# Expert rows written to a buffer of their own and added in the last stage, slots read from DRAM tables, down biases added once per token

## The chip, the cores and the metric

One core of a Trainium2 chip runs the whole program. The metric is the time of one execution in microseconds of the device; lower is better. A run of the kernel before is repeated on the same chip, and the median counts. One execution was also taken with the hardware profiler, and the trace comes from that one.

The names of the engines in the profile: PE does matrix products and transposes, DVE works on vectors, ACT does activations and copies with a scale, POOL does small work and issues the indirect transfers, SP issues loads.

## The reference, cut to what matters

A float32 transformer of two blocks on 512 tokens of 1024 columns. The second block has 32 experts, of which every token takes 4. What the change touches is the expert part and what follows it:

```python
xn = rms_norm_2(h, ffn_norm)
logits = xn @ w_router + b_router
top_vals, top_idx = lax.top_k(logits, 4)
gates = softmax(top_vals)
# for each expert e, on the rows of the tokens that chose it
gt = minimum(xb @ w_gate[e] + b_gate[e], 7.0)
up = clip(xb @ w_up[e] + b_up[e], -7.0, 7.0)
hdn = (up + 1.0) * (gt * sigmoid(1.702 * gt))
y = (hdn @ w_down[e] + b_down[e]) * gate
h = h + sum over a token's four experts of y
gate = sigmoid(rms_norm_2(h, ple_gate_norm) @ w_ple_gate)
h = h + gate * rms_norm_2(p @ w_ple_proj, ple_post_norm)
```

## The kernel before, in words

Every large product is made in three matmuls on a pair of reduced operands (`mm3`, lines 314 to 316): high x high, low weight x high, high weight x low. A weight part is 128 rows of 1024 columns: one load on SP (line 296), a cast to the high part `whi` on ACT (line 285), a subtraction that leaves the low part `wlo` on DVE (line 285), and six matmuls of 512 columns on PE.

**Routing.** `attended_rows(tt)` ends the attention's output for a token tile of 128 (tiles 3, 2, 1, 0 in turn), writes it to `base` in DRAM on ACT's queue, and `route(tt)` (line 1293) finds the four experts: transposes, the router matmuls (line 1309), `rstd` on POOL (lines 320, 323), `lg`, the top four, `chosen`, and a running count of tokens per expert, which is each token's slot (`slot_of`). `info` keeps for every token and expert the gate in two parts, the token number and the row's norm in two parts. After the last tile `first_rows` makes the token numbers `gi` of expert 0, and POOL gathers its rows from `base` (line 1424).

**Slots.** The list of tokens of an expert comes from a product: a one-hot matrix of the slots (`one_hot`, DVE, line 1419) times `info` (`slot_products`, four small matmuls, line 1489), copied out and turned into the gate and the row numbers (`slot_columns`). Experts 0 and 1 are done ahead of the loop, the other 30 in groups of four inside it, at every fourth expert.

**The expert loop** (line 1586). An expert has 112 slots. Its 24 steps `q` are: q 0 to 7 the gate product into `pg`, q 8 to 15 the up product into `pu`, q 16 to 23 the down product of the expert before into `pd`. At q 0, 8 and 16 `add_bias` (line 1465) starts the sum with the bias, by two matmuls of 512 columns on `pick`. `turned` transposes the gathered rows `xg` after q 15 and the hidden rows `uc` after q 23 (line 1511, eight transposes each); `halves_of` splits them into `xe` (q 17) and `he` (q 1). `limited_up` and `gated_rows` make `uc` on DVE at q 18 and 19; for expert 0, which has no q 16 to 23, they stand at its end. `put_rows` scales the down product by the gate (`yt`, ACT) and adds it to the tokens' rows of `base`, by an indirect transfer that accumulates (POOL, line 1527). `fetch` keeps four parts ahead.

The order on PE, DVE and ACT inside the loop is the order of the program text, made fast by dependences after the loop. SP loads in the order of the parts, as raw buffers come free. POOL issues the gathers and the writes in its own fixed order.

**The last stage** loads each tile's finished row from `base` (`hk`, line 1751) and the product of p (`ee`), transposes it, multiplies by the gate weights (four tiles of 48 matmuls), and writes out. Two runs of warming matmuls (`keep_warm`, line 364) keep PE busy between the loop and the last stage.

## Time and profile before

| what | us |
|---|---|
| median of 3 runs (2210.2 to 2211.66) | 2210.4 |
| profiled execution, its own time | 2211.0 |
| span of the profiled execution | 2209.3 |
| PE busy | 2116.2 (96%) |
| DVE busy | 1650.9 (75%) |
| ACT busy | 1357.8 (61%) |
| POOL busy | 207.0 (9%) |

The span runs from the first to the last recorded instruction; what lies around it, 1.7 us, is in the run's own time. The busy share of PE is a mean over stages: the first block and the attention up to about 860 us, the routing up to 924, the expert loop up to 2127, and the last stage. A row of the timeline gives the start, the busy time, engine, line, operation, the tile written and those read, and in brackets the idle time before with what ended it. Matmuls overlap, so the step from one start to the next is their pace, not their busy time. Lines are those of the kernel before.

### The profile page before, as it was taken

The numbers are of one execution on the slowest core, as the hardware profiler recorded it, in microseconds if no ns is written. First come the engines' busy times: TensorE is split into PE (matmuls) and PEld (weight loads), VectorE is DVE, ScalarE is ACT, GpSimd is POOL, SyncE is SP. The second block draws the span as 40 slices with busy tenths as digits, with TensorE's granted clock in tenths as the row PEclk, the third lists the DMA queues.
The fourth block names the chain that finished last, engine by engine and source line by source line (L and its number), as shares of the span: only waits on it lengthen the run. The fifth ranks groups of instructions, "written<-read, shape, count | busy, mean of one in ns | idle before, by whom it ended". The sixth has DMA issues, their size and how long they took to land. (4 is left out here: it accounts for less than half of the span.)

```text
span 2209.3 us, 29934 instructions
## 1 busy us (share of the span) xinstructions
PE 2116.2 (96%) x10458; PEld 1670.1 (76%) x10459; DVE 1650.9 (75%) x2291; ACT 1357.8 (61%) x1841; POOL 207.0 (9%) x325
## 2 busy tenths in 40 slices
PE   9999999999999889799999999999999999999997
PEld 7777788888878777567777777777777777777776
DVE  6688772223576756778888989898889888888852
ACT  5666652222564644367777777777777777777851
POOL 0000110000003332100000000000000000000010
PEclk9999999999999989899999999999999999999999
DMA  6401744333664025689999999999999999999751
GB/s 212 152 30 30 263 145 154 96 96 123 217 210 130 11 96 205 240 294 347 358 338 368 335 364 342 361 344 355 345 357 342 360 352 344 352 357 350 265 165 38
DMA packets 159977, 543.75 MB, mean 246 GB/s; under 512 B 23107, under 2 KB 26179, under 8 KB 159820
## 3 DMA queue, kind: packets, MB, share of 16 engines
q1 hardware_dynamic: 138816, 500.63, 62.9%
q0 software_dynamic: 8192, 16.80, 3.6%
q10 hardware_dynamic: 12812, 24.35, 3.2%
q8 instruction: 84, 1.38, 0.3%
q14 instruction: 73, 0.60, 0.1%
HBM read 525.93 MB, written 28.33 MB: 251 GB/s over the span
## 5 line engine op out<-in xcount | busy, mean ns | idle before, releaser
L285 DVE TENSOR_TENSOR wlo<-wraw,whi 128x1024 fp32r<-128x1024 f32 x923 | 1101.2, 1221 | 315.5 <-ACT whi L285 288.2
L285 ACT CAST whi<-wraw 128x1024 fp32r<-128x1024 f32 x923 | 955.6, 1051 | 407.0 <-PE pw L316 243.7
L314 PE MATMUL pw<-whi,xe 128*112 128x512 f32 x1024 | 405.8, 396 | 0.2 <-ACT xe L285 0.2
L316 PE MATMUL pw<-whi,xe 128*112 128x512 f32 x1024 | 402.4, 393 | 1.1 <-DVE xe L285 1.1
L315 PE MATMUL pw<-wlo,xe 128*112 128x512 f32 x1024 | 402.0, 393 | 0.0
L316 PEld LDWEIGHTS pw<-whi,xe 128*112 128x112 f32 x1024 | 178.6, 174 | 60.1 <-DVE xe L285 1.6
L315 PEld LDWEIGHTS pw<-wlo,xe 128*112 128x112 f32 x1024 | 179.3, 175 | 55.6
L314 PEld LDWEIGHTS pw<-whi,xe 128*112 128x112 f32 x1024 | 178.8, 175 | 56.0 <-ACT xe L285 0.4
L315 PE MATMUL pw<-wlo,he 128*112 128x512 f32 x512 | 203.4, 397 | 18.1 <-DVE wlo L285 18.1
L314 PE MATMUL pw<-whi,he 128*112 128x512 f32 x512 | 202.0, 394 | 0.4 <-ACT he L285 0.4
L316 PE MATMUL pw<-whi,he 128*112 128x512 f32 x512 | 201.0, 393 | 0.0
L315 PEld LDWEIGHTS pw<-wlo,he 128*112 128x112 f32 x512 | 89.3, 174 | 61.9 <-DVE wlo L285 36.5
L314 PEld LDWEIGHTS pw<-whi,he 128*112 128x112 f32 x512 | 89.2, 174 | 29.2 <-ACT he L285 0.8
L1527 POOL DMA_INDIRECT base<-yt,gi x32 | 54.2, 1694 | 595.8 <-ACT yt L1583 595.8
L316 PEld LDWEIGHTS pw<-whi,he 128*112 128x112 f32 x512 | 89.3, 174 | 26.3 <-DVE he L285 0.4
L1424 POOL DMA_INDIRECT xg<-normed,gi x31 | 32.6, 1051 | 530.3 <-PE tr L1511 530.3
L320 POOL TENSOR_SCALAR rstd<-ss 128x1 f32<-128x1 f32 (+1 forms) x68 | 25.0, 368 | 608.2 <-DVE ss L865 387.4
L314 PE MATMUL pa<-x2T,whi 128*128 128x512 f32 (+1 forms) x200 | 72.6, 364 | 0.1
L315 PE MATMUL pa<-x2T,whi 128*128 128x512 f32 (+1 forms) x200 | 72.7, 364 | 0.0
L316 PE MATMUL pa<-x2T,wlo 128*128 128x512 f32 (+1 forms) x200 | 72.6, 363 | 0.0
L1467 PE MATMUL pw<-bias,pick 128*112 128x512 f32 x192 | 65.2, 421 | 0.0
L314 PE MATMUL pb<-whi,x3T 128*128 128x256 f32 x192 | 56.0, 292 | 0.0
(540 smaller groups left out, 3656.5 us busy)
## 6 DMA issues: line engine op xcount, KB each, us to landing
wraw<-in_we_gate_dram SPq DMA_DIRECT2D x256, 512.0 KB, 5.8
wraw<-in_we_up_dram SPq DMA_DIRECT2D x256, 512.0 KB, 6.6
wraw<-in_we_down_dram SPq DMA_DIRECT2D x256, 512.0 KB, 6.9
wraw<-in_w_gu_dram SPq DMA_DIRECT2D x44, 512.0 KB, 3.7
wraw<-in_w_down_dram SPq DMA_DIRECT2D x44, 512.0 KB, 3.9
wraw<-in_w_out_dram SPq DMA_DIRECT2D x24, 512.0 KB, 6.1
wraw<-in_w_v_dram SPq DMA_DIRECT2D x10, 512.0 KB, 4.0
wraw<-in_w_uv_dram SPq DMA_DIRECT2D x8, 512.0 KB, 4.3
```

Of the source, the lines that this page charges most:

```text
L285: return nc.scalar.copy(hi, src), nc.vector.tensor_tensor(out=lo, in0=src, in1=hi.bitcast(F32), op=ALU.subtract)
L314: nc.tensor.matmul(o, a[0], b[0], start=start, stop=False)
L315: nc.tensor.matmul(o, a[0], b[1], start=False, stop=False)
L316: W["mm"] = nc.tensor.matmul(o, a[1], b[0], start=False, stop=stop)
L320: ins = nc.gpsimd.tensor_scalar(out=r[:, :w], in0=ss, scalar1=1.0 / n, scalar2=eps, op0=ALU.mult, op1=ALU.add)
L1424: nc.gpsimd.indirect_dma_start(out=xg[:CAP], out_offset=None, in_=normed if e else base, in_offset=bass.IndirectOffsetOnAxis(ap=slots[e][1 ...
L1467: nc.tensor.matmul(ps[:CAP, c * 512:(c + 1) * 512], pick[:, j % 2, e:e + 1].to_broadcast([P, CAP]), bias[:, j // 2, c * 512:(c + 1) * 512] ...
L1527: nc.gpsimd.indirect_dma_start(out=base, out_offset=bass.IndirectOffsetOnAxis(ap=ap, axis=0), in_=y_, in_offset=None, bounds_check=S - 1, ...
```

## The change

Four things are changed, and some are moved with them.

1. `put_rows` writes its rows plainly to `ybuf`, 2048 rows, four for each token (`store_rows`); nothing accumulates. The last stage loads a token's four rows (`yb`) beside the row of `base` and adds them, on DVE and, for tiles 1 to 3, one addition of each half on POOL.
2. Experts 2 to 31 get their slots from DRAM. 16 tables are set to zero early on SP; after each tile's routing POOL scatters 128 entries of 16 bytes (gate, token, row number) into one table for each of the four choices; SP loads all 16 back, and `finish_table` sums them on DVE in expert 1 at q 3. The one-hot products stay for experts 0 and 1 only.
3. The down bias leaves the loop: the gates are transposed once (expert 2, q 10) and multiplied by all down biases for each token tile in the last stage (`add_down_biases`).
4. `uc` of expert 0 is made at q 0 and 1 of expert 1, and every `uc` is transposed at q 6 of the next expert and split at q 8. The gather of expert 2 stands at q 4 of expert 1. The load of `g_ffn_norm` moves to a pool of its own, behind the attention. Five pools are released at other places.

```diff
+        ybuf = dram.tile([4 * S, D], F32, name="ybuf")
+
+        tables = [dram.tile([P * NE, 4], F32, name=f"table{j}") for j in range(4 * NT)]
+        zeros = mixq.tile([P, 4 * NE], F32, name="zeros")
+        nc.gpsimd.memset(zeros, 0.0)
+        for t in tables:
+            nc.sync.dma_start(t.rearrange("(s e) c -> s (e c)", e=NE), zeros)
...
+        entry = rt.tile([P, NT, 4, 4], F32, name="entry")
+        nc.gpsimd.memset(entry, 0.0)
+        nc.vector.tensor_copy(entry[:, :, :, 1], tok1[:, :, None].to_broadcast([P, NT, 4]))
+        nc.vector.tensor_copy(entry[:, :, :, 2], row)
+        gate_of = rt.tile([P, NT, NE], F32, name="gate_of")
+
+        gateT = rt.tile([P, S], F32R, name="gateT")
...
+            e2 = rp.tile([P, 4, NE], F32, tag="eq2", name="eq2", bufs=1)
+            nc.vector.tensor_tensor(out=e2, in0=eq, in1=slot_of[:, tt, None, :].to_broadcast([P, 4, NE]), op=ALU.mult)
+            at = rp.tile([P, 4], F32, tag="at", name="at", bufs=2)
+            nc.vector.reduce_sum(at, e2, axis=AX)
+            nc.vector.scalar_tensor_tensor(out=place[:, tt], in0=at, scalar=float(NE), in1=ixf, op0=ALU.mult, op1=ALU.add)
...
+        for j, t in enumerate(tables):
+            nc.gpsimd.indirect_dma_start(out=t, out_offset=bass.IndirectOffsetOnAxis(ap=place[:, j // 4, j % 4:j % 4 + 1], axis=0), in_=entry[:, j // 4, j % 4], in_offset=None,
+                                         bounds_check=P * NE - 1, oob_is_err=False)
...
+        def prepare_slots(e):
+            row_column(info[:, :, e, 0], float(e), early)
+            pt = ps_tr()
+            oh = one_hot(e) if e else oh0[0]
             for tt in range(NT):
-                W["pick"] = nc.tensor.matmul(pt[:CAP, 6 * j:6 * j + 6], oh[:, tt], info[:, tt, e], start=tt == 0, stop=tt == NT - 1)
-
-        def slot_columns(pt, e0, n):
-            sl = early.tile([P, NB, 6], F32, name="sl", bufs=2)[:CAP, :n]
-            nc.vector.tensor_copy(sl.rearrange("p j c -> p (j c)"), pt[:CAP, :6 * n])
-            *cols, last = slot_rows(early, sl, n, 4, CAP, e0 == 0)
-            for j in range(n):
...
+        def table_slots():
+
+            tab = early.tile([P, NE, 4], F32, name="tab")
+            sums = []
+            for h in range(2):
+                t = row_tile("tabs").rearrange("p (j f) -> p j f", j=8)
+                for j in range(8):
+                    nc.sync.dma_start(t[:, j], tables[8 * h + j].rearrange("(s e) c -> s (e c)", e=NE))
+                sums.append(t)
+
+            def finish():
+                flat = tab.rearrange("p e c -> p (e c)")
+                part = early.tile([P, 4 * NE], F32, name="tab2")
+                for o, t in zip((flat, part), sums):
+                    nc.vector.reduce_sum(o, t.rearrange("p j f -> p f j"), axis=AX)
+                nc.vector.tensor_tensor(out=flat, in0=flat, in1=part, op=ALU.add)
+                gi, si, _ = rows_of(early, tab[:, :, 1], tab[:, :, 2], NE)
+                for e in range(2, NE):
+                    slots[e] = (tab[:CAP, e, 0:1], gi[:CAP, e:e + 1], si[:CAP, e:e + 1], None)
+
+            return finish
 
         def turned(a):
 
...
-        def add_rows(y_, ap):
-
-            nc.gpsimd.indirect_dma_start(out=base, out_offset=bass.IndirectOffsetOnAxis(ap=ap, axis=0), in_=y_, in_offset=None,
-                                         bounds_check=S - 1, oob_is_err=False, compute_op=ALU.add)
+                scale_rows(xg[:CAP, cs], xg[:CAP, cs], slots[0][3], gpre[:CAP, cs])
+
+        def store_rows(y_, ap):
+            nc.gpsimd.indirect_dma_start(out=ybuf, out_offset=bass.IndirectOffsetOnAxis(ap=ap, axis=0), in_=y_, in_offset=None,
...
         for e in range(NE):
-            if e + 1 < NE:
-                gather(e + 1)
-            batch = list(range(e + 2, min(e + 2 + NB, NE))) if e % NB == 0 else []
-            ohs, pts, pslot = {}, None, None
+            pts, pgate = None, None
             for q in range(24 if e else 16):
                 fetch(at["i"] + 4)
+                if e == 1 and q == 3:
+                    finish_table()
+                if q == (4 if e == 1 else 0) and e + 1 < NE:
+                    gather(e + 1)
                 if q == 0:
                     hidden["pg"] = ps_wide()
                     add_bias(hidden["pg"], e, 0)
-                if q == 1 and e:
-                    operand["h"] = halves_of(turned_h, "he")
+                if e == 1 and q in (0, 1):
+                    (limited_up, gated_rows)[q]()
                 if q == 2 and pd is not None:
                     put_rows(e - 2, pd)
                     pd = None
-                if q in (0, 2, 6, 8) and len(ohs) < len(batch):
-                    ohs[len(ohs)] = one_hot(batch[len(ohs)])
-                if q in (4, 6, 10, 12):
-                    j = (4, 6, 10, 12).index(q)
-                    if j < len(batch):
-                        if j == 0:
-                            pslot = ps_tr()
-                        slot_products(pslot, j, ohs[j], batch[j])
-                if q == 13 and batch:
-                    slot_columns(pslot, batch[0], len(batch))
+                if q == 6 and e:
+                    turned_h = turned(hidden["u"])
                 if q == 8:
+                    if e:
+                        operand["h"] = halves_of(turned_h, "he")
                     hidden["pu"] = ps_wide()
                     add_bias(hidden["pu"], e, 1)
                 if q == 10:
                     limited_gate()
+                    if e == 2:
+                        pgate = turn_gates()
+                if q == 12 and e == 2:
+                    split_gates(pgate)
                 if q == 16:
                     pd = ps_wide()
-                    add_bias(pd, e - 1, 2)
                 if q == 17 and e + 1 < NE:
                     operand["x"] = halves_of(pts, "xe")
                 if q == 18:
...
                 if q < 16:
                     product(hidden["pg" if q < 8 else "pu"], operand["x"])
                 else:
-                    product(pd, operand["h"])
+                    product(pd, operand["h"], q == 16)
                 if q == 15 and e + 1 < NE:
                     pts = turned(xg[:CAP])
             if e == 0:
                 operand["x"] = halves_of(pts, "xe")
-                limited_up()
-                gated_rows()
-            turned_h = turned(hidden["u"])
         put_rows(NE - 2, pd)
-        operand["h"] = halves_of(turned_h, "he")
+        operand["h"] = halves_of(turned(hidden["u"]), "he")
         pd = ps_wide()
-        add_bias(pd, NE - 1, 2)
         for q in range(8):
             fetch(at["i"] + 4)
-            product(pd, operand["h"])
+            product(pd, operand["h"], q == 0)
         last = W["mm"]
         put_rows(NE - 1, pd)
...
+        def add_down_biases(tt, h):
+
+            ps = ps_wide()
+            for cs in (slice(0, 512), slice(512, D)):
+                nc.tensor.matmul(ps[:, cs], gateT[:, tok(tt)], bdown[:, cs], start=True, stop=True)
+            nc.vector.tensor_tensor(out=h, in0=h, in1=ps, op=ALU.add)
...
+            def load_rows(tt, parts):
+                ybs[tt] = wp.tile([P, 4, D], F32, name="yb")
+                for c in range(parts):
+                    cs = slice(c * D // parts, (c + 1) * D // parts)
+                    load(ybs[tt][:, :, cs], yv[tok(tt), :, cs])
...
+            load_rows(0, 4)
+            hs = dict(enumerate(hs))
+            load_row(hs, 1, base)
+            load_rows(1, 2)
+            load_row(es, 0, ed)
...
+                if tt + 2 < NT:
+                    load_row(hs, tt + 2, base)
+                    load_rows(tt + 2, 2)
+                if tt + 1 < NT:
+                    load_row(es, tt + 1, ed)
+                h, e, yb = hs[tt], es[tt], ybs[tt]
+                if tt:
+                    add_down_biases(tt, h)
                 xT = [wp.tile([P, 8, P], F32R, name=f"x4T{j}") for j in range(2)]
-                transposed(h, xT, slice(0, P), step=4)
...
+                for cs in cols:
+                    for z in range(2):
+                        nc.vector.tensor_tensor(out=h[:, cs], in0=h[:, cs], in1=yb[:, z, cs], op=ALU.add)
+                    eng = nc.gpsimd if tt else nc.vector
+                    eng.tensor_tensor(out=yb[:, 2, cs], in0=yb[:, 2, cs], in1=yb[:, 3, cs], op=ALU.add)
+                    nc.vector.tensor_tensor(out=h[:, cs], in0=h[:, cs], in1=yb[:, 2, cs], op=ALU.add)
+                transposed(h, xT, slice(0, P), step=8 // max(parts, 2))
```

On POOL, in the routing, at tile 2's `info` (casts and subtractions of `rstd`) and tile 1's `rstd` behind it. Before:

```order
L320 TENSOR_SCALAR rstd<-ss 128x1
L323 TENSOR_TENSOR rstd<-rstd,mhalf 128x1
L1312 CAST info<-rstd 128x32
L1313 TENSOR_TENSOR info<-rstd,info 128x32
L320 TENSOR_SCALAR rstd<-ss 128x1
L323 TENSOR_TENSOR rstd<-rstd,mhalf 128x1
L1312 CAST info<-rstd 128x32
L1313 TENSOR_TENSOR info<-rstd,info 128x32
L1424 DMA xg<-base,gi_8967 112x1024
```

Now, from tile 2's `info` on:

```order
L1333 TENSOR_TENSOR info<-rstd,info 128x32
L1478 DMA table_8106<-entry,place 4096x4
L1478 DMA table_8107<-entry,place 4096x4
L1478 DMA table_8108<-entry,place 4096x4
L1478 DMA table_8109<-entry,place 4096x4
L1478 DMA table_8102<-entry,place 4096x4
L1478 DMA table_8103<-entry,place 4096x4
L1478 DMA table_8104<-entry,place 4096x4
L319 TENSOR_SCALAR rstd<-ss 128x1
L1478 DMA table_8105<-entry,place 4096x4
L322 TENSOR_TENSOR rstd<-rstd,mhalf 128x1
```

Tile 3's four scatters (tables 8106 to 8109) and tile 2's four (8102 to 8105) have come between tile 2's `info` and the end of tile 1's `rstd`. Four more, of tile 1, stand ahead of the first gather (`xg<-base`), and tile 0's four between it and the second.

On PE, where expert 0 ends and expert 1 begins. Before:

```order
L316 MATMUL pw<-whi,xe_9086 112x512
L1511 MATMUL tr<-ident,xg 128x112 x8
L1511 MATMUL tr<-ident,uc 128x112 x8
L1467 MATMUL pw<-bias,pick 112x512 x2
L314 MATMUL pw<-whi,xe_9331 112x512
```

Now:

```order
L315 MATMUL pw<-whi,xe_9231 112x512
L1564 MATMUL tr<-ident,xg 128x112 x8
L1494 MATMUL pw<-bias,pick 112x512 x2
L313 MATMUL pw<-whi,xe_9443 112x512
L314 MATMUL pw<-wlo,xe_9443 112x512
```

The transposes of `uc` have left this place; they stand 36 matmuls later.

On DVE, at the same place. Before:

```order
L285 TENSOR_TENSOR wlo<-wraw,whi 128x1024 x2
L285 TENSOR_TENSOR xe_9332<-tr,xe_9331 128x448 x2
L1575 TENSOR_SCALAR uc<-pw 112x1024
L1579 SCALAR_TENSOR_TENSOR uc<-gm,uc 112x1024
L285 TENSOR_TENSOR wlo<-wraw,whi 128x1024 x2
```

Now:

```order
L284 TENSOR_TENSOR wlo<-wraw,whi 128x1024 x15
L284 TENSOR_TENSOR xe_9444<-tr,xe_9443 128x448 x2
L284 TENSOR_TENSOR wlo<-wraw,whi 128x1024
L1632 TENSOR_SCALAR uc<-pw 112x1024
L284 TENSOR_TENSOR wlo<-wraw,whi 128x1024
L1636 SCALAR_TENSOR_TENSOR uc<-gm,uc 112x1024
L284 TENSOR_TENSOR wlo<-wraw,whi 128x1024 x2
L1549 TENSOR_REDUCE tab<-tabs 128x128
L1549 TENSOR_REDUCE tab_9497<-tabs 128x128
L1550 TENSOR_TENSOR tab<-tab,tab_9497 128x128
```

A `wlo` of expert 1 stands behind `xe` and behind each of the two `uc`, and the sums of the tables come two parts later.

## Rows read from the trace of the kernel before

**Rows 1.** Busy time by stretch: us, busy us (count) of each engine, PE clock, DMA share, GB/s.

```profile
840.00:924.00 84.00, 68.21 (x355) 53.56 (x353) 54.14 (x165) 27.34 (x68) 16.43 (x33) 0.88 0.62 223
1200.00:1300.00 100.00, 98.19 (x462) 74.58 (x461) 89.50 (x89) 73.77 (x81) 6.42 (x5) 1.00 0.98 348
2143.00:2146.00 3.00, 2.92 (x12) 2.12 (x13) 1.29 (x2) 1.67 (x4) 0.00 (x0) 1.00 1.00 388
```

**Rows 2.** Waits of the expert loop, 924 to 2128: us in total, times, longest.

```profile
ACT whi L285 <- PE pw L316: 243.7, 418, 8.1
...
PE pw L315 <- DVE wlo L285: 18.1, 30, 0.6
```

**Rows 3.** Waits of the load queue on SP, same stretch.

```profile
SPq L296 <- DVE wlo L285: 846.6, 729, 6.1
```

**Rows 4.** Timeline of PE inside the loop, 1503 to 1526.

```profile
1505.16 0.69 PE L1467 MATMUL pw<-bias,pick 128*112 128x512 f32 x2
1505.69 0.39 PE L314 MATMUL pw<-whi,he 128*112 128x512 f32 x1
...
1524.42 0.46 PE L1489 MATMUL tr<-info,oh 128*112 128x6 f32 x4
...
1525.28 0.39 PE L316 MATMUL pw<-whi,xe 128*112 128x512 f32 x1
1525.51 0.39 PE L314 MATMUL pw<-whi,xe 128*112 128x512 f32 x1
```

**Rows 5.** Timeline of PE from expert 0 to expert 1.

```profile
949.99 0.93 PE L1511 MATMUL tr<-ident,xg 112*128 112x112 f32 x8
955.39 1.73 PE L1511 MATMUL tr<-ident,uc 112*128 112x112 f32 x8 [4.47 <-DVE uc L1579]
...
957.77 0.63 PE L314 MATMUL pw<-whi,xe 128*112 128x512 f32 x1
...
961.04 0.40 PE L316 MATMUL pw<-whi,xe 128*112 128x512 f32 x1
```

**Rows 6.** Timeline of DVE, routing and experts 0 and 1.

```profile
900.02 1.28 DVE L340 SCALAR_TENSOR_TENSOR hx<-hx,rstd,g_ffn_norm 128x1024 f32<-128x1024 f32 x1 [4.39 <-DMA base<-hx]
...
915.25 0.38 DVE L1345 TENSOR_REDUCE gg<-eq 128x32 f32<-128x128 f32 x1
...
951.71 1.15 DVE L285 TENSOR_TENSOR xe<-tr,xe 128x448 fp32r<-128x448 f32 x2
...
955.16 1.22 DVE L285 TENSOR_TENSOR wlo<-wraw,whi 128x1024 fp32r<-128x1024 f32 x1
```

**Rows 7.** Timeline of POOL in the routing.

```profile
893.51 0.19 POOL L320 TENSOR_SCALAR rstd<-ss 128x1 f32<-128x1 f32 x1 [6.76 <-ACT junk L329]
...
904.51 0.19 POOL L320 TENSOR_SCALAR rstd<-ss 128x1 f32<-128x1 f32 x1 [9.51 <-ACT junk L329]
...
915.59 1.28 POOL L1424 DMA_INDIRECT xg<-base,gi  x1 [9.60 <-DVE gi L1436]
```

**Rows 8.** Page, costliest groups: count, busy, mean ns, idle before with releaser.

```profile
L1527 POOL DMA_INDIRECT base<-yt,gi x32 | 54.2, 1694 | 595.8 <-ACT yt L1583 595.8
...
L1424 POOL DMA_INDIRECT xg<-normed,gi x31 | 32.6, 1051 | 530.3 <-PE tr L1511 530.3
```

**Rows 9.** DMA queues, 962 to 2085: packets, MB, share of 16 engines.

```profile
DMA packets 111021, 392.98 MB, mean 350 GB/s; under 512 B 15256, under 2 KB 15256, under 8 KB 110941
...
q1 hardware_dynamic: 103517, 376.96, 90.6%
q0 software_dynamic: 7424, 15.03, 6.4%
```

**Rows 10.** Timeline of PE between the loop and the last stage.

```profile
2136.04 5.73 PE L364 MATMUL tr<-whi 128*128 128x512 f32 x24 [2.31 <-PEq L1737]
2141.61 1.04 PE L348 MATMUL tr<-ident,hk 128*128 128x128 f32 x8
```

**Rows 11.** Timeline of ACT at the same place.

```profile
2139.89 1.06 ACT L329 ACTIVATE junk<-hk 128x1024 bf16<-128x1024 f32 x1 [6.28 <-DMA hk<-base]
```

More of the change, by code (lines that the diff above doesn't have):

```diff
@@ L1404, in build @@
         xg = early.tile([P, D], F32, name="xg")
-        bias = early.tile([P, 2, D], F32R, name="bias")
+        bias = early.tile([P, D], F32R, name="bias")
         pick = early.tile([P, 2, NE], F32R, name="pick")
@@ L1431, in first_rows @@
             for tt in range(NT):
-                nc.tensor.matmul(pt[:CAP, 0:2], oh0[0][:, tt], info[:, tt, 0, 2:4], start=tt == 0, stop=tt == NT - 1)
+                nc.tensor.matmul(pt[:CAP, 0:2], oh0[0][:, tt], info[:, tt, 0, 3:5], start=tt == 0, stop=tt == NT - 1)
             gi = early.tile([P, 2], I32, name="gi0", bufs=1)[:CAP]
@@ new lines, in prepare_slots @@
+        def prepare_slots(e):
+            row_column(info[:, :, e, 0], float(e), early)
+            pt = ps_tr()
+            oh = one_hot(e) if e else oh0[0]
+            for tt in range(NT):
+                W["pick"] = nc.tensor.matmul(pt[:CAP, 0:6], oh[:, tt], info[:, tt, e], start=tt == 0, stop=tt == NT - 1)
+            sl = early.tile([P, 6], F32, name="sl", bufs=2)[:CAP]
+            nc.vector.tensor_copy(sl, pt[:CAP, :6])
+            sg, rr, gi, si, last = slot_rows(early, sl, CAP, 2)
+            slots[e] = (sg, gi, si, rr)
+            return last
@@ L1553, in build, with product @@
         at = {"i": 0}
-        def product(ps, a):
+        def product(ps, a, first=False):
             i = at["i"]
@@ new lines, in build, with load @@
+            es, ybs = {}, {}
+            chain = []
+            def load(dst, src):
+                ins = nc.sync.dma_start(dst, src)
+                if chain and len(chain) < 9:
+                    hold(ins, chain[-1])
+                chain.append(ins)
+            def load_rows(tt, parts):
[3 more added lines that the diff above has]
+                    load(ybs[tt][:, :, cs], yv[tok(tt), :, cs])
```

136 lines of the change are left out of this document (80 added, 56 removed).

## The prediction, before the changed kernel had run

> **What bounds the kernel now.** I read three views first: the busy times by stretch, the waits of the expert loop, and the timeline of PE at the places that the change touches. In the stretches one sees PE matmuls busy for 98.19 of 100 us in the middle of the loop, DVE for 89.50 and the DMA engines for 0.98, at a full clock; in the routing stretch ahead of it PE has 68.21 of 84 us, so latencies count there [rows 1]. In the waits one sees that the large ones are upstream of PE: ACT's casts wait 243.7 us for PE to free a buffer, while PE itself waits 18.1 us for DVE, 30 times [rows 2]. The load queue waits 846.6 us for DVE to free raw buffers [rows 3]. So PE sets the loop's pace, and a matmul taken out of it is time gained, as long as DVE and the loads can follow. The profiled run took 2211.0 us, 0.6 above the median of 2210.4; the sum below is made against 2211.0 and then lowered by 0.6.
>
> **The change, part by part.**
>
> *Down bias out of the loop.* Its two matmuls start at 1505.16 and the first product of the down stage at 1505.69, so they hold PE for 0.53 us [rows 4]. 31 experts pay it; the last one's pair lies in a wait for its operand. I take 0.5 each: **-15.5**.
>
> *Slot products out of the loop.* Four small matmuls start at 1524.42; the third product matmul behind them starts at 1525.28, 0.86 us later, where two steps at the usual 0.23 (1525.28 to 1525.51) would be 0.46 [rows 4]. So a group costs 0.40; 30 groups leave the loop: **-12.0**. With them go DVE's 30 one-hot operations. I give that nothing by itself, since PE, not DVE, sets the pace.
>
> *The seam from expert 0 to expert 1.* Before, PE ends its first eight transposes and waits 4.47 us for DVE's uc; from 949.99 to 961.04 it takes 11.05 us, of which two groups of transposes (0.93 each), a bias (0.5) and eight product matmuls (8 x 0.23) are needed, 4.2 in all: 6.9 are lost, part of them because those eight take 3.27 (957.77 to 961.04) and not 1.84 [rows 5]. Now the uc transposes stand 36 matmuls later, and DVE takes uc between two wlo of expert 1. What is late next: PE wants xe's low part at about 951.9 (949.99 + 0.93 + 0.5 + 2 x 0.23), and DVE ends it at 952.86 (951.71 + 1.15) [rows 6], some 0.5 to 1 us. Then DVE has extra work before its wlo: xe 1.15, two uc at the price of a wlo (1.22), and the table sums (two reductions over 128x1024, no row of this shape, bounded below by 1.22 each and above by the 0.38 for 128 elements taken eight times, 3.0 each; I take 1.3, near the row with the same tile size, plus about 1 for the small ones). That is 7.2 us, against a lead of four parts of 6 x 0.23, 5.5 us [rows 4, 6]. So PE waits 1 to 3 us more: 3.4 of the 6.9 come back, **-3.5** (ends: +1 with the dear reductions, -6 without a wait).
>
> *Routing.* Three things lengthen it. (1) DVE: two larger and one small operation more per token tile (the reduction 0.38 [rows 6], the product not more, the last less), and three small ones for each of two experts in front of gi of expert 0: about 1.5 us on the way to the first gather. (2) POOL: eight scatters now stand between tile 2's info and the end of tile 1's rstd, where POOL idled 6.76 us, and four before the first gather, where it idled 9.60 after an idle 9.51 [rows 7]. No row has a 16-byte scatter; the nearest are the gather, 1.05, and the accumulating write, 1.69 [rows 8], so eight take 8.4 to 13.5 us, and the last ones can't start before tile 2's gates are there. Tile 1's rstd comes 3 to 7 us later. The DVE behind it waited 4.39 us for a DMA anyway [rows 6]. (3) In the order of DVE tile 0's scaling, which waits for tile 0's write to land and for its rstd, now stands ahead of tile 1's chosen, and PE's router products for tile 0 behind that. Together: **+5**, between 0 (all of it inside the two waits) and +12 (1.69 each and no cover). SP's queue is passed too: 16 table loads stand ahead of expert 1's last weights, but expert 1 begins only at 957.77 [rows 5], 42 us after the first gather, so I give them nothing; were the last scatter to land later than that, they would cost the difference.
>
> *Written plainly.* The 31 writes inside the loop become plain. q0 took 6.4% of the DMA time for 15.03 MB, where the loads' rate (90.6% for 376.96 MB) would make it 3.6% [rows 9]: at most 2.8% of 1123 us comes free, 31 us of DMA time, and at least none. On PE's path it counts nothing in the sum, since the loads wait for buffers.
>
> The Trainium skill, "DMA: Bandwidth & Descriptors", section Specifications, speaks against the tables: below 512 B a transfer is a read-modify-write and not at line rate. These pieces are 16 B, and the trace of before shows none; by that rule the time would move towards that of the scatters' rival below, by rows 7 and 8 it stays at the sum.
>
> *Gates turned, and the biases at the end.* Four transposes are half of 0.93: **+0.5**. Two matmuls for each of four token tiles at 0.26: **+2.1** [rows 4, 5].
>
> *The last stage.* Before, the warming matmuls start at 2136.04 and take 5.73, and the transposes follow at 2141.61, though the row of h was there at 2139.89 [rows 10, 11]: 1.7 us of cover. Now 2 MB more come per token tile, in four pieces for the first one. At the 388 GB/s of this stage [rows 1] a piece of 0.5 MB takes 1.35 us, and DVE's four additions of 128x256 not over 1.7 (a third of a wlo's 1.22 each [rows 6]). So the first piece is ready some 1 us after the warming, and the next ones come faster than PE's 12 matmuls each (2.8 us). **+1**, from 0 to +7, if short rows halve the rate and the second tile is late.
>
> The sum: -15.5 - 12.0 - 3.5 + 5 + 0.5 + 2.1 + 1 = **-22.4**, 2188.6 against 2211.0, so **2188** against the median.
>
> **The rivals.**
>
> *The loads are at their limit (slower).* The loop's middle moves 350 GB/s at a DMA share of 0.98 [rows 1, 9]. Without 25 of its 1123 us the 392.98 MB need 358 GB/s. If a load can't land faster and plain writes take what accumulating ones took, the 27.5 us turn into waits of ACT and DVE for wraw, and only the other terms are left: +5 + 0.5 + 2.1 + 1 - 3.5 = +5.1, **2215.5**. It decides below about 352 GB/s: at 351.6 the middle of the loop takes 1117.7 us, 5.3 less than 1123, which just pays for them. For it: the share of 0.98, and waits for loads that are there already. Against it: 388 GB/s at a share of 1.00 in the last stage [rows 1], and a load queue that waits for buffers [rows 3]. Chance 0.10, half of it short of a slower kernel.
>
> The Trainium skill, "DMA: Bandwidth & Descriptors", section Specifications, gives about 358 GB/s for a core's share of HBM. By that the loop would come out at 1098 us, just where I put it; the 388 of rows 1 do not agree with it as a ceiling.
>
> *The scatters hold POOL (slower).* If one of them takes over 4 us, the twelve ahead of the first gather take 48 us, 28 more than at the dearest row, and every gather and rstd behind them on POOL is late by that: 2188 + 28 = **2216**. At 3.9 each the gain is just eaten. For it: no row has the operation. Against it: 1.05 and 1.69 [rows 8]. Chance 0.05.
>
> *DVE becomes the bound.* DVE has 89.50 busy of 100 already [rows 1] and keeps its chain of xe and two uc in the down stage, which makes the 18.1 us. If half of the 27.5 comes back as such waits: **2202**. Against it: per expert DVE loses the one-hot too, so its share rises by less than a point. Chance 0.15.
>
> *More than forecast.* The front is covered by the two waits and the seam closes fully: -5 - 2.5, **2180.5**. Chance 0.10.
>
> **How the numbers follow.** The forecast has 0.60, with a range of its own from 2182 to 2196. The range reaches to DVE's case and to the better one with the open ends of front and tail: **2177 to 2206**, leaving out nearly all of the loads' and the scatters' cases. About 0.2%, 4.4 us, is what a measurement can tell from no change. Faster than that: 0.60 + 0.10 + 0.15 = 0.85. Within it: 0.05, the loads' case halfway. Slower: 0.05 + 0.05 = 0.10.
>
> **What would show it.** Right: experts that follow each other some 0.86 us sooner (27.5 over 32), PE's groups for the down bias and the slot products gone, its wait for wlo near 18 us, q0's share lower, no 4.5 us wait at the seam, the first gather about 5 us later than 915.59 [rows 7], tiles of the last stage some 0.5 us longer. Wrong: casts that wait for weights by more than they do now, a gather of expert 0 over 12 us later, a last stage over 7 us longer, or PE's waits for wlo up by 10 us or more.

## The result, and the profile after

The changed kernel takes 2192.95 us (median of 4 runs, 2190.05 to 2195.03), the kernel before 2210.86 beside it: a ratio of 0.992, 95% interval 0.990 to 0.9935. That is 17.9 us less, where 22.4 were forecast. The profiled execution of the changed kernel is the longest of the four: 2195.03, with a span of 2193.3 against 2209.3, 16.0 less.

Two marks on PE divide the two spans: the first product of expert 0 (924.30 before, 934.20 now), and the first of the warming matmuls behind the loop (2126.73, 2107.60).

| stretch | before | now | measured | forecast |
|---|---|---|---|---|
| start to expert 0's first product | 924.30 | 934.20 | +9.9 | +5 |
| expert loop, to the warming | 1202.43 | 1173.40 | -29.0 | -30.5 (-15.5 - 12.0 - 3.5 + 0.5) |
| warming to the end of the span | 82.57 | 85.70 | +3.1 | +3.1 (2.1 + 1) |

So in these two traces the loop and the end came nearly as forecast, and the front cost twice what it was given.

**The loop.** The timeline of PE, the transposes of the gathered rows of three experts that follow each other; first the kernel before:

```profile
1504.46 0.93 PE L1511 MATMUL tr<-ident,xg 112*128 112x112 f32 x8
...
1543.17 0.93 PE L1511 MATMUL tr<-ident,xg 112*128 112x112 f32 x8
...
1580.16 0.93 PE L1511 MATMUL tr<-ident,xg 112*128 112x112 f32 x8
```

and the changed kernel:

```profile
1499.33 0.93 PE L1564 MATMUL tr<-ident,xg 112*128 112x112 f32 x8
...
1535.80 0.93 PE L1564 MATMUL tr<-ident,xg 112*128 112x112 f32 x8
...
1572.28 0.93 PE L1564 MATMUL tr<-ident,xg 112*128 112x112 f32 x8
```

Before, an expert with slot products took 38.71 us (1504.46 to 1543.17) and the next one, without, 36.99. Now both take 36.48 (36.47 and 36.48). The difference of the two kinds, 1.6 to 1.7 for four groups, is the 0.40 per group of [rows 4]; the other 0.51 is the down bias.

The waits of the loop in the changed kernel, 924 to 2115, those of ACT and PE (us in total, times, longest):

```profile
ACT whi L284 <- PE pw L315: 192.3, 389, 4.3
...
PE pw L314 <- DVE wlo L284: 20.5, 31, 2.7
```

and of the load queue on SP:

```profile
SPq L295 <- DVE wlo L284: 804.9, 719, 6.1
```

ACT still waits mostly for PE, 192.3 us for 243.7 [rows 2], and the load queue for buffers, 804.9 for 846.6 [rows 3]: PE still sets the pace, with less lead. PE's wait for `wlo` has grown only by one entry of 2.7, at the seam. The page of the changed kernel, its costliest groups, has the other 30, and the indirect transfers:

```profile
span 2193.3 us, 29698 instructions
...
L314 PE MATMUL pw<-wlo,he 128*112 128x512 f32 x512 | 204.2, 399 | 17.8 <-DVE wlo L284 17.8
...
L1450 POOL DMA_INDIRECT xg<-normed,gi x31 | 32.3, 1041 | 564.2 <-PE tr L1564 508.8
...
L1579 POOL DMA_INDIRECT ybuf<-yt,si x32 | 30.9, 967 | 550.0 <-ACT yt L1640 550.0
```

A plain write holds POOL for 967 ns, the accumulating one 1694 [rows 8]. The DMA queues in the middle of the changed loop, 972 to 2072 us (packets, MB, share of 16 engines):

```profile
DMA packets 111529, 394.48 MB, mean 359 GB/s; under 512 B 15390, under 2 KB 15390, under 8 KB 111452
...
q1 hardware_dynamic: 103772, 377.84, 92.6%
q0 software_dynamic: 7680, 15.69, 4.4%
```

Nearly the same bytes as in [rows 9] (392.98 MB) went at 359 GB/s instead of 350, and q0's share fell from 6.4 to 4.4%.

**The seam** from expert 0 to expert 1, the changed kernel's PE (answers to [rows 5]):

```profile
958.47 0.93 PE L1564 MATMUL tr<-ident,xg 112*128 112x112 f32 x8
...
960.90 0.49 PE L315 MATMUL pw<-whi,xe 128*112 128x512 f32 x1 [0.54 <-DVE xe L284]
...
971.02 0.39 PE L313 MATMUL pw<-whi,xe 128*112 128x512 f32 x1
974.08 0.77 PE L314 MATMUL pw<-wlo,xe 128*112 128x512 f32 x1 [2.67 <-DVE wlo L284]
974.65 0.63 PE L315 MATMUL pw<-whi,xe 128*112 128x512 f32 x1
975.08 0.63 PE L313 MATMUL pw<-whi,xe 128*112 128x512 f32 x1
...
976.36 0.90 PE L1494 MATMUL pw<-bias,pick 128*112 128x512 f32 x2
977.09 0.40 PE L313 MATMUL pw<-whi,xe 128*112 128x512 f32 x1
```

The 4.47 us wait is gone; 0.54 and 2.67 stand in its place, and behind the second one PE goes at 0.43 per matmul (1.2 GHz: the granted clock is 0.50 from 974 to 976) instead of 0.23 until 976.36. From these transposes to the next expert's, at 988.21, it is 29.74 us, against 31.81 before (949.99 to 981.80): 2.1 gained. The wait comes from DVE, which makes the two table sums here (its timeline):

```profile
968.10 3.89 DVE L1549 TENSOR_REDUCE tab<-tabs 128x128 f32<-128x1024 f32 x2
```

**The front.** The last scaling of the attention's output (`ob`) on DVE starts at 879.30, before at 873.71: 5.6 us of the 9.9 are lost before the routing has begun. (Counted from the end of the first block, the row `tn<-pa,rstd,g_norm_ffn_post` of DVE at 669.40, before at 670.52, `ob` comes after 209.90 us instead of 203.19: 6.7 later.) The rest, 4.3, lies between it and expert 0 (54.9 us for 50.6). The timeline of DVE in the changed kernel, from that scaling to the first one of the routing (answers to [rows 6]):

```profile
879.30 0.35 DVE L339 SCALAR_TENSOR_TENSOR ob<-po,rstd,sub 128x128 f32<-128x128 f32 x1 [2.09 <-POOL rstd L322]
...
886.65 1.28 DVE L339 SCALAR_TENSOR_TENSOR hx<-hx,rstd,g_ffn_norm 128x1024 f32<-128x1024 f32 x1 [3.04 <-DMA g_ffn_norm<-in_ffn_norm_dram]
```

That of POOL (answers to [rows 7]), scatters ahead of tile 1's `rstd`, and the first gather:

```profile
905.78 0.97 POOL L1478 DMA_INDIRECT table<-entry,place  x1 [5.54 <-DVE place L1360]
907.06 0.97 POOL L1478 DMA_INDIRECT table<-entry,place  x1 [0.30 <-issue]
...
925.58 1.04 POOL L1450 DMA_INDIRECT xg<-base,gi  x1 [2.65 <-DVE place L1360]
```

A scatter takes 1.28 us of POOL (905.78 to 907.06); the first gather is 10.0 later than in [rows 7]. Why the attention ends later is seen in two places. SP's queue, at the start of the second block:

```profile
669.55 5.77 SPq L1263 DMA_DIRECT2D table<-zeros  x7
675.43 0.39 SPq L295 DMA_DIRECT2D wraw<-in_w_qk_dram  x1
675.87 8.41 SPq L1263 DMA_DIRECT2D table<-zeros  x9
```

Meanwhile ACT, which issues small loads on its own queue, stands still, here for one of 4 KB (`rcol`). In e1, which stores the zeros later, its wait at the same cast is for PE and half as long (timelines of ACT, changed kernel and e1). It is 5.1 to 6.7 us in the six traces with the stores at this place and 2.5 in all others:

```profile
680.37 1.08 ACT L284 CAST x3T<-tr 128x512 fp32r<-128x512 f32 x2 [5.35 <-DMA rcol<-in_col_ffn_norm_dram]
...
675.60 1.25 ACT L284 CAST x3T<-tr 128x512 fp32r<-128x512 f32 x2 [2.51 <-PE tr L347]
```

The second place is ACT near the attention's end:

```profile
869.09 1.04 ACT L284 CAST bdown<-wraw 32x1024 fp32r<-32x1024 f32 x1
870.16 1.05 ACT L1474 CAST bdown<-wraw 32x1024 fp32r<-32x1024 f32 x1
871.23 0.37 ACT L284 CAST wT<-tr 128x256 fp32r<-128x256 f32 x1
```

The 16 zero stores take 14.2 us of SP's queue among the second block's weights, and two casts for the down biases run on ACT ahead of a `wT`, which the attention of the last tiles needs.

### The profile page after: what moved, and what is told of

Its sections match the earlier page's. It is cut to its first block, busy times and chain, and to the rows that moved or that the text cites. A ratio compares the mean times of both kernels' runs of the same rounds, so it can differ in the third digit from the quotient of the medians.

```text
span 2193.3 us, 29698 instructions
## 1 busy us (share of the span) xinstructions
PE 2096.8 (96%) x10286; PEld 1656.8 (76%) x10287; DVE 1663.0 (76%) x2300; ACT 1363.3 (62%) x1846; POOL 210.2 (10%) x351
## 5 line engine op out<-in xcount | busy, mean ns | idle before, releaser
L284 ACT CAST whi<-wraw 128x1024 fp32r<-128x1024 f32 x923 | 957.0, 1050 | 373.7 <-PE pw L315 192.3
L314 PE MATMUL pw<-wlo,he 128*112 128x512 f32 x512 | 204.2, 399 | 17.8 <-DVE wlo L284 17.8
L313 PE MATMUL pw<-whi,he 128*112 128x512 f32 x512 | 203.2, 397 | 0.9 <-ACT he L284 0.9
L1579 POOL DMA_INDIRECT ybuf<-yt,si x32 | 30.9, 967 | 550.0 <-ACT yt L1640 550.0
L314 PE MATMUL pb<-wlo,x3T 128*128 128x256 f32 x192 | 56.8, 296 | 0.0
```

The lines of the kernel that those rows point to most:

```text
L284: return nc.scalar.copy(hi, src), nc.vector.tensor_tensor(out=lo, in0=src, in1=hi.bitcast(F32), op=ALU.subtract)
L313: nc.tensor.matmul(o, a[0], b[0], start=start, stop=False)
L314: nc.tensor.matmul(o, a[0], b[1], start=False, stop=False)
L1579: nc.gpsimd.indirect_dma_start(out=ybuf, out_offset=bass.IndirectOffsetOnAxis(ap=ap, axis=0), in_=y_, in_offset=None, bounds_check=4 * S - ...
```

## The experiments

The theory: the loop's terms are as forecast, the plain writes give PE nothing, and what the front lost came from the zero stores and the routing. The rivals: the loads are at their limit, so that cheaper writes paid; the scatters hold POOL; the steps of the loop were worth something else. Medians are of 4 to 10 runs; every run of the kernel before beside them lies between 2210.47 and 2211.54 as median. The runs e1 to e4, e0 with e5 to e7, and e8 to e11 are from three chips, each with the kernel before beside them. Each experiment is an edit of the changed kernel unless another is named.

**e0, unedited.** The changed kernel again.

> The changed kernel once more, unedited, on the chip of the next three: 2190 to 2195. Its first expert product should start between 930 and 934.5, as in the three runs with the same front (934.20, 931.07, 930.39): that spread is what one profile of the front tells.

2194.12 (2192.96 to 2197.13), interval 0.991 to 0.9945. Expert 0's first product stands at 932.27, the loop takes 1173.36, the end 87.57. The loop repeats to a tenth; front and end move by 2 us from run to run. An effect there below about 2 us can't be told from one run.

**e1, zero stores late:** held behind the matmul ahead of them in the text; in the trace they stand at 823.32 to 839.6 us.

```diff
-            nc.sync.dma_start(t.rearrange("(s e) c -> s (e c)", e=NE), zeros)
+            hold(nc.sync.dma_start(t.rearrange("(s e) c -> s (e c)", e=NE), zeros), W["mm"])
```

> The 16 stores of zeros go behind the loads of the out projection on SP, into a stretch (about 840 us) in which the DMA share was 0.25; nothing else is edited. Theory: ahead of the second block's loads they make the attention 2.5 us late (in the changed kernel the same step of DVE is level at 675.8 us and 2.57 late at 678.4, right behind seven of the stores), and that delay is carried to the first expert. Then the first expert product starts 2 to 3 us earlier than 934.2 and the time is about 2190.5. Rival: the delay is absorbed in the attention and made again by the routing's own waits; then the product starts within 1 us of 934.2 and the time is within 1 us of the changed kernel's 2193.

2189.02, interval 0.988 to 0.992: 3.9 below the changed kernel. The second block's `x3T` is made at 676.69 instead of 680.99, and `ob` starts at 875.71 instead of 879.30. Expert 0's first product stands at 928.16, 6.0 earlier where 2 to 3 were expected; from the first block's end to `ob` it is 206.92 us for 209.90. The theory held, with a larger effect.

**e2, scatters late:** all 16 held behind the first gather on POOL.

```diff
+            W["gathered"] = nc.gpsimd.indirect_dma_start(out=xg[:CAP], ...
-            nc.gpsimd.indirect_dma_start(out=t, ...
+            hold(nc.gpsimd.indirect_dma_start(out=t, ...), W["gathered"])
```

> All 16 scatters go behind the first gather on POOL; with that the order of DVE has tile 0's scaling behind tile 1's chosen again, as in the kernel before. Theory: the eight scatters ahead of tile 1's rstd hold POOL from 899 to 911 us, most of it blocked on tile 2's place, and DVE waits for rstd behind them; without them the first gather is issued about 5 us earlier than 925.6 (919 to 922) and the time is about 2188. Rival: the write of tile 0's rows to DRAM and the late gain row set the routing's pace, so the first gather comes within 1.5 us of 925.6 and the time is 2191 to 2194. Second rival: the tables then land too late for expert 1, and a wait of DVE for the tables or of casts for expert 1's weights appears in 945 to 985 us, over 3 us long.

2190.92, interval 0.989 to 0.992, 2.0 lower. The step from `ob` to expert 0 is 50.1 instead of 54.9. The edit moves two things: the scatters, and with them DVE's order, in which tile 0's scaling stands behind tile 1's `chosen` again. The last stage takes 89.9; part of that is the second piece of `yb`, for which DVE waits 2.99 us (1.03 in the changed kernel). By itself unclear, so e5 and e10 repeat the edit beside a kernel without it.

**e3, down bias back in the loop** (it adds the gate's bias a second time, two matmuls of the same size):

```diff
                     pd = ps_wide()
+                    add_bias(pd, e - 1, 0)
...
-                    product(pd, operand["h"], q == 16)
+                    product(pd, operand["h"])
```

> Two bias matmuls are put back ahead of each of the 31 down stages of the loop (they add the gate bias, so the output has that added; the one at the end for all biases stays). Theory: PE sets the pace, so the loop is 31 x 0.5 = 15.5 us longer, time about 2208.5, and nothing else moves. Rival (DVE or loads set part of the pace): under 8 us longer, with PE's waits for wlo or the casts' waits for weights shorter by the rest.

2206.20, interval 0.997 to 0.9986; the loop takes 1185.54, 12.1 more. An expert takes 36.94 instead of 36.48, 0.46, near the forecast's 0.5; 31 times that is 14.3. PE kept 2.4 GHz at the seam in this run (28.43 us there instead of 29.74), and expert 0's products took 0.8 less, which hides 2.1 of the sum. The term holds, at nine tenths of its size.

**e4, slot products back in the loop,** with a result that nothing reads:

```diff
+                if q in (4, 6, 10, 12):
+                    j = (4, 6, 10, 12).index(q)
+                    if j < len(batch):
+                        pslot = ps_tr()
+                        for tt in range(NT):
+                            nc.tensor.matmul(pslot[:CAP, 0:6], oh0[1][:, tt], info[:, tt, batch[j]], start=tt == 0, stop=tt == NT - 1)
```

> 30 groups of four small slot matmuls are put back at the places they had in the kernel before, on expert 1's one-hot matrix and with a result that nobody reads; DVE's one-hot operations are not put back. Theory: 30 x 0.40 = 12 us longer, time about 2205. Rival: the small matmuls fill gaps in which PE would wait anyway, under 6 us longer.

2203.29, interval 0.9945 to 0.997; the loop takes 1185.02, 11.6 more, 0.39 for each of 30 groups. The term held.

**e5, e1 and e2 together.**

> Both edits of the two front runs together: zeros behind the out projection's loads, scatters behind the first gather. Theory (two separate delays): the step from the last attention scaling to the first expert product is 50 us as with the late scatters alone (the kernel before has 50.6), and the attention is as early as with the late zeros (last scaling about 875.7), so the first product starts at 925.5 to 926.5 and the time is 2186 to 2188. Rival (one delay, seen from two sides): no earlier product than 926 and a time not under the 2189.0 of the late zeros.

2190.73, interval 0.989 to 0.992: no better than e1 alone. My expectation that late scatters would add to it fell. The step from `ob` to expert 0 is 51.1 for 52.45 in e1, but the loop takes 1176.28 for 1171.50: in expert 0 PE waits for weights three times (0.36, 0.60 and 0.77), as it doesn't in e1, and the clock falls at the seam.

**e6, e5 with all of the last stage's additions on DVE:**

```diff
-                    eng = nc.gpsimd if tt else nc.vector
+                    eng = nc.vector
```

> As the run with both edits, and the additions of the last stage that stood on POOL (tiles 1 to 3, half a row each, two per tile) go to DVE. Theory: in the changed kernel DVE's additions of 128x512 take 1.2 us beside POOL's and 0.68 alone, so POOL's work is not free: with all on DVE a tile has six additions of 0.68 and tile 1's second half of x4T is no later; the tail is 0.5 to 1.5 us shorter, time 0.5 to 1.5 below the run with both edits. Rival: DVE has that much more to do, and the tail is longer by the two additions per tile, 1.4 us for tile 1.

2187.04, interval 0.987 to 0.991, and the end takes 83.23 instead of e5's 87.42: 4.2 less, more than expected. The changed kernel's timelines: two additions on DVE in one row, the second of them by itself (the timeline from 2130.77 on), POOL's that starts during the first, and one of DVE's alone:

```profile
2130.06 2.39 DVE L1863 TENSOR_TENSOR hk<-hk,yb 128x512 f32<-128x512 f32 x2
...
2130.79 1.67 DVE L1863 TENSOR_TENSOR hk<-hk,yb 128x512 f32<-128x512 f32 x1
...
2130.39 1.51 POOL L1865 TENSOR_TENSOR yb<-yb 128x512 f32<-128x512 f32 x1 [0.45 <-DVE x4T L284]
...
2147.11 0.68 DVE L1863 TENSOR_TENSOR hk<-hk,yb 128x512 f32<-128x512 f32 x1
```

and the same addition in e6:

```profile
2127.24 0.69 DVE L1863 TENSOR_TENSOR hk<-hk,yb 128x512 f32<-128x512 f32 x1
```

Alone an addition takes 0.69 us. The one that starts while POOL's runs takes 1.67 and ends 0.56 after POOL's (2132.46, POOL's at 2131.90); the 1.2 of the expectation is the mean of the pair. So giving POOL one in four lengthened DVE's part: its three took 3.2 us from 2130.06 on, and the four of e6 2.6. PE's wait for `x4T` at tile 1 was 3.04 in e5 and is 0.90 here, and the products behind it start 2.0 us earlier. The other 2.2 of the 4.2 are the clock: those products up to tile 2's take 14.84 us in e5, at a granted clock of 0.84, and 12.65 here, at 1.00. The Trainium skill, "SBUF — State Buffer", section "SBUF: two separate sides", says that VectorE and GpSimd take turns on a port pair and one blocks for the other's whole instruction; the rows agree: DVE's addition ends only after POOL's.

**e7, 29 accumulating writes beside the plain ones** (the sums then hold experts 0 to 28 twice):

```diff
+            if e < NE - 3:
+                nc.gpsimd.indirect_dma_start(out=base, out_offset=bass.IndirectOffsetOnAxis(ap=slots[e][1], axis=0), in_=yt, in_offset=None,
+                                             bounds_check=S - 1, oob_is_err=False, compute_op=ALU.add)
```

> The changed kernel, and experts 0 to 28 write their rows a second time, adding them to the rows of base as the kernel before did (so the sums hold those experts twice). Theory: loads wait for buffers and PE sets the pace, so the expert loop stays within 1.5 us of the changed kernel's 1173.4, although q0's share of the DMA time rises by over 4 points. Rival: the loads are at their limit; 29 accumulating writes of about 0.46 MB are then paid for: over 10 us longer, with the casts' waits for weights (67 us in the loop) up by about that.

2189.73, interval 0.989 to 0.992. The DMA queues of e7, 972 to 2072:

```profile
DMA packets 114725, 400.10 MB, mean 364 GB/s; under 512 B 17219, under 2 KB 17219, under 8 KB 114646
...
q1 hardware_dynamic: 103254, 375.96, 90.5%
q0 software_dynamic: 11392, 23.18, 7.7%
```

q0 has more than the kernel before had (7.7% for 6.4; 3.3 points above the changed kernel, where over 4 were expected), and the loop still takes 1171.73, no longer than the changed one's 1173.40 (PE kept 2.4 GHz at the seam, which is most of the 1.7). So the writes' DMA time is hidden, and the loads were not at their limit at 359 GB/s. The whole run is 4.4 below e0, by some 1.5 each in front, loop and end; nothing in the edit accounts for that.

**e8, a version that draws on these:** e1, all additions on DVE, and the two casts of the down biases, with the subtraction on DVE that goes with them, held behind the first gather.

```diff
-        split(braws[2], bdown[0:NE], bdown[2 * NE:3 * NE])
-        nc.scalar.copy(bdown[NE:2 * NE], braws[2])
...
+        for ins in (*split(braws[2], bdown[0:NE], bdown[2 * NE:3 * NE]), nc.scalar.copy(bdown[NE:2 * NE], braws[2])):
+            hold(ins, W["gathered"])
```

> The changed kernel with three edits: zeros late, all additions of the last stage on DVE, and the two casts and the subtraction of the down biases (bdown) moved behind the routing. Theory: with the zeros late the last attention scaling comes at 875.5 to 875.8 in three profiles and at 873.71 in the kernel before; the 2 us left are the two bdown casts (1.04 and 1.05) that stand ahead of a wT cast on ACT, so it now comes at 873.5 to 874, the last stage takes 83 as with the additions on DVE, and the time is 2183 to 2185.5. Rival: ACT had room there and the rest of the attention's delay has another cause; then the scaling stays at 875.5 or later and the time is 2185.5 or more.

2183.75 (2182.71 to 2190.78), interval 0.987 to 0.991. `ob` starts at 871.93, 3.8 before e1's, and earlier than in the kernel before. Not all of that is the casts: the first block already ends 0.8 earlier (`tn` at 668.01, in e1 at 668.79), which the edit doesn't touch. The casts show in the last two tiles: their two steps of `ob` together take 9.26 us here and 11.20 in e1 (9.35 in the kernel before). ACT now goes straight to `wT` (its timeline in e8):

```profile
863.50 0.27 ACT L284 CAST mixB<-tr 128x128 fp32r<-128x128 f32 x1 [1.78 <-PE tr L1222]
864.64 0.37 ACT L284 CAST wT<-tr 128x256 fp32r<-128x256 f32 x1 [0.87 <-PE tr L1209]
```

**e9, e8 with the gain row loaded by SP,** not by ACT's queue:

```diff
-        gpre = gain_row("ffn_norm_2", gp)
+        gpre = gp.tile([P, D], F32, name="g_ffn_norm_2", bufs=1)
+        nc.sync.dma_start(gpre, I["ffn_norm_2"][0].partition_broadcast(P))
```

> As the run with three edits, and the gain row g_ffn_norm is loaded by SP, ahead of expert 0's last weights, instead of by ACT between its casts. In the changed kernel DVE waits 3.04 us for it, 8.6 us after its issue at a DMA share of 0.93. Theory: the late gain row is what the routing lost; issued ahead of the weights it lands before DVE wants it, and the step from the last scaling to the first expert product falls from 52.5 to about 50. Rival: SP is held by the same pool release, and the row comes no earlier; then the step stays within 1 us and only the weights come later.

2181.81 (2181.4 to 2184.2), interval 0.985 to 0.989: the best version, 28.7 below the kernel before. The first scaling of the routing has no wait for the gain row, which took 3.04 in the changed kernel; but it has none in e8 either, with the load still on ACT's queue. DVE's timeline in e8, then in e9:

```profile
877.23 1.28 DVE L339 SCALAR_TENSOR_TENSOR hx<-hx,rstd,g_ffn_norm 128x1024 f32<-128x1024 f32 x1
...
879.64 0.25 DVE L1334 SCALAR_TENSOR_TENSOR lg<-po,rstd,g_b_router 128x32 f32<-128x32 f32 x1
879.80 1.27 DVE L339 SCALAR_TENSOR_TENSOR hx<-hx,rstd,g_ffn_norm 128x1024 f32<-128x1024 f32 x1
```

The step from `ob` to expert 0 is 49.5, for 52.9 in e8, but the routing also runs in another order: DVE's four scalings stand 6.8, 19.2, 22.1 and 34.3 us behind `ob`, in e8 5.3, 17.8, 29.8 and 38.4. So the theory, that the late gain row is what the routing lost, is not shown. And e9's time is 1.9 below e8's, within what front and end move by themselves.

**e10, e8 with the scatters late** (the edit of e2).

> As the run with three edits, with the scatters behind the first gather as well. The two profiles of late scatters without other edits of the routing had steps of 50.1 and 51.1 us from the last scaling to the first expert product, a third 53.9, those with early scatters 52.2 to 54.9. Theory (scatters on POOL are paid for): 1 to 2 us below the run with three edits. Rival: what the first gather gains is lost again in expert 0, where PE waited 0.4 + 0.6 + 0.8 us for weights around 946 to 951 in two of the runs with both edits late; then the time is within 1 us of it.

2186.56, interval 0.9875 to 0.991, not below e8, where 1 to 2 us were expected: `ob` to expert 0 takes 50.3 for 52.9, and it doesn't show in the time. In e5 and in e10 the scatters' place on POOL was worth nothing that can be measured.

**e11, e9 with the table sums spread** over q 4, 7 and 9 of expert 1, and the gather of expert 2 at q 9, since it needs them:

```diff
-                if e == 1 and q == 3:
-                    finish_table()
-                if q == (4 if e == 1 else 0) and e + 1 < NE:
+                if e == 1 and q in (4, 7, 9):
+                    finish_table((4, 7, 9).index(q))
+                if q == (9 if e == 1 else 0) and e + 1 < NE:
```

> As the run with the gain row on SP, and the table sums of expert 1 are spread: one reduction at q 4, one at q 7, the rest at q 9, with the gather of expert 2 behind it at q 9 instead of q 4. Theory: DVE's extra work at the seam is paid as far as it exceeds the lead of four parts; the wait of 2.67 us (in all ten profiles of this front 2.65 to 2.71), and the low clock that follows it in half of them, 1.7 us more, shrink to waits of 1 us or less at 2.4 GHz: loop about 1170 to 1171.5, time 2179 to 2181. Rival: the gather of expert 2 comes too late for its transposes, and a wait for xg of over 1 us appears at the end of expert 1's up product; then the time is 2181 or more.

2185.62, interval 0.987 to 0.990: nothing gained, 3.8 above e9. The 2.7 us wait at the seam split into three of 0.6 or less, 1.2 in all, but a new one came (PE's timeline in e11):

```profile
976.37 1.73 PE L1567 MATMUL tr<-ident,xg 112*128 112x112 f32 x8 [3.57 <-DMA xg<-normed,gi]
```

The gather, put later, was late. The sums at one place were not a mistake: they bring the gather in time.

## Why the prediction was right, and where it was off

The direction, the range (2177 to 2206) and the mechanism hold: PE set the pace of the loop, and matmuls taken out of it came back nearly one for one. By its steps:

- *Down bias, -15.5.* Held: 0.51 per expert between the two traces, 0.46 put back in e3.
- *Slot products, -12.0.* Held: 1.6 to 1.7 for four groups, and 11.6 put back in e4.
- *Seam, -3.5.* Measured -2.1. The waits are as forecast ("0.5 to 1" was 0.54, "1 to 3" was 2.67), although the reductions took 1.95 each and not 1.3 (its bounds were 1.22 and 3.0). What is missing is the stretch at 1.2 GHz behind the wait; runs without it show 28.43 us for the seam, 3.4 gained.
- *Routing, +5.* **This is the step that was mis-sized: +9.9,** and from 6.1 to 9.9 in the runs with that front. Its own three parts are not the cause: between `ob` and expert 0 the changed kernel, e0, e1, e3, e4 and e7 lose 1.6 to 4.3 us. The step left out what the change puts ahead of the routing. It went past SP's queue for the 16 table loads alone, not for the 16 zero stores, which hold up ACT's small loads, and it never priced the casts of the down biases on ACT. From the first block's end (`tn`) to `ob` the changed kernel, e0, e3, e4 and e7 take 209.6 to 210.2 us (e2, with the same stores, 207.7), e1, e5 and e6 206.4 to 206.9, e8 to e10 203.9 to 204.4, the kernel before 203.2. So the stores cost some 3 us and the casts 2.4, of which 1.9 stand in the last two tiles: 11.2 us there in all nine traces with the casts in that place, 9.3 in e8 to e11. A wait of 2.7 to 3.2 at the routing's first scaling, in five of the nine traces of the changed kernel and e0 to e7 put down to the gain row (its load is issued 8.6 us ahead, before 63.6), is a third that the step didn't name; what it cost isn't shown, as it is gone in e8 and e10 with the load issued 6.5 us ahead.
- *Scatters.* 1.28 us each on POOL, in the forecast's bracket of 1.05 to 1.69, and nothing in the time (e10). (The rival's "3.9 each" is a slip: by its own figures the gain is eaten at 3.6.) By the Trainium skill's rule on transfers under 512 B ("DMA: Bandwidth & Descriptors", Specifications) the time would have gone towards the scatters' rival, 2216; it didn't.
- *Written plainly, 0.* Held: e7.
- *Gates turned, end biases, last stage, +3.6.* The sum came out (the expert with the gates takes 36.99 for 36.48, +0.51; the end +3.1), the last stage's part of it by luck. From mark to mark on PE, tile 0's products up to tile 1's take 2.2 us more, the wait for `x4T` in tile 1 adds 1.1, tile 2's take 1.7 less, and the last tile and what follows 1.6 more. Most of that is where the clock falls, which the forecast did not have. Tile 2's products up to tile 3's, before and now (busy times by stretch; the number behind POOL's is the granted clock):

```profile
2175.13:2189.49 14.36, 13.35 (x55) 10.65 (x55) 1.62 (x3) 1.80 (x4) 0.00 (x0) 0.88 0.07 27
...
2159.23:2171.88 12.65, 11.64 (x54) 9.49 (x54) 6.44 (x10) 2.94 (x6) 0.74 (x2) 1.00 0.22 72
```

  Tile 0's went the other way, from a clock of 1.00 (13.53 us) to 0.90 (15.76, with the new bias matmuls). DVE's additions beside POOL's are in it too: e6's end, with all of them on DVE, is 2.5 us shorter than the changed kernel's and 4.2 shorter than e5's.

The rivals: the loads at their limit, refuted by e7 and by 359 GB/s, above the 352 at which it was to decide. (The Trainium skill's 358 GB/s, same page and section, is not a ceiling here either: e7 shows 364 over 1100 us.) One sign of being wrong did come: the casts wait 67.0 us for weights in the loop, 47.0 before. It didn't reach PE, and e7, with more traffic, has 42.3. The scatters on POOL, refuted by their 1.28 us each, and by e5 and e10. DVE as the bound: PE's waits for `wlo` in the loop stayed at 17.8. "More than forecast" did not come from the changed kernel. e8 and e9, at 2183.75 and 2181.81, come near its 2180.5, with the front covered as its condition has it (expert 0's first product at 924.80 and 922.43, before at 924.30), but with a seam that didn't close and a last stage helped by e6's edit.

Open: what moves front and end of the same kernel by 2 us from run to run. In the end it shows at one place: e0's wait for `x4T` in tile 1 is 3.04 us for 1.98 in the changed kernel, and the products behind it take 14.79 for 14.29; why that wait differs, no run here tells.

## What to carry to other kernels

Where one engine sets the pace, an instruction taken off it is worth about its step in the timeline (the bias pair: 0.53 read, 0.51 gained, 0.46 when put back); the price of the change lies in the preparations that such a change puts elsewhere (here stores of zeros and casts of constants), each ahead of work that is waited for. Go through every queue from the first instruction that the change adds, not from the stage that it is about. And put preparation where its engine waits anyway: here that and the additions kept on DVE were together worth 11 us (e9), where the change itself had brought 17.9. Before a difference of 2 us is put down to an edit, look at the granted clock and at the order of the instructions in both traces: an edit can move either.

## What was not expected of the hardware

**The clock after the same wait.** The seam's wait, 2.65 to 2.71 us (2.98 in e4), is in twelve traces: the changed kernel's and those of e0 to e10. In the changed kernel, e0, e2, e4, e5 and e9 some matmuls behind it go at 0.43 us each, 1.2 GHz (granted clock 0.50), and the seam takes 29.61 to 30.00 us; in e1, e3, e6, e7, e8 and e10 they stay at 0.23, 2.4 GHz (1.00), and it takes 28.42 to 28.44. Rows of PE in e6, to set beside those of the changed kernel above:

```profile
967.82 0.39 PE L313 MATMUL pw<-whi,xe 128*112 128x512 f32 x1
970.88 0.49 PE L314 MATMUL pw<-wlo,xe 128*112 128x512 f32 x1 [2.67 <-DVE wlo L284]
971.21 0.40 PE L315 MATMUL pw<-whi,xe 128*112 128x512 f32 x1
971.44 0.39 PE L313 MATMUL pw<-whi,xe 128*112 128x512 f32 x1
```

The same idle time in the same work, and the clock falls in half of the traces: 1.2 to 1.6 us, and nothing in the edits sorts the two halves.

**POOL's help that costs.** An addition of 128x512 on DVE takes 0.69 us alone and 1.2 to 1.8 when it starts during one on POOL (the changed kernel, e0 and e5, tile 1).
